# Convolution tails traced in stages, recurrence stages every third step, and the last layer norm's vectors loaded in pieces

## The chip, the cores and the metric

The kernel runs on one core of a Trainium2 chip. The metric is device time in microseconds (us) of the whole program, the median of several runs. TensorE (PE in the profile) multiplies matrices, VectorE (DVE), ScalarE (ACT) and GpSimd (POOL) work elementwise, and the queue of SyncE (SP, SPq where its sequencer issues) issues nearly all DMA loads.

## The reference

One decoder block on 256 tokens of width 2048, in float32:

```python
h = layer_norm(x, emb_ln_g, emb_ln_b)
p = h @ w_in                                   # a, gate, q, f, i, og
u = causal_dwconv(a * sigmoid(gate), conv_w)   # 31 taps, 1024 channels
u = silu(group_layer_norm(u))                  # 8 groups of 128
o = hgrn2_recurrence(silu(q), 1 - fg, i, log(fg))   # 8 heads, fg from f
o = rms_norm(o) * hgrn_norm_g * silu(og)
h = layer_norm(ALPHA * h + concat(u, o) @ w_out, ln1_g, ln1_b)
g, v = split(h @ w_ffn_up)                     # 5632 each
h = layer_norm(ALPHA * h + (silu(causal_dwconv(g)) * v) @ w_ffn_down, ln2_g, ln2_b)
```

## The kernel before

**Weights.** All weights come as 392 blocks of 128 x 1024 floats, 512 KB each, in the order in which they are used. `load_halves` (L97) keeps up to four loads (`raw`, L101) traced ahead on SP's queue. Each block is split into a rounded part `wh` (ScalarE, L124) and a rest `wl` (VectorE, L127), so that products of two rounded halves keep float32's accuracy.

**Products.** `mm_features` (L288) makes 256 features for all tokens from four blocks: `high` (L274) multiplies `wh` with both halves of the input, `low` (L281) `wl` with the high half. `mm_tokens` (L360) makes 512 features with the tokens as the stationary operand, 12 matmuls (L356 to L358) a step of two blocks of the inner dimension.

**Order.** The kernel is written for a scheduler that lays out each engine's instructions ahead of time: the earlier an instruction is traced, the earlier it stands, as far as its inputs are ready by the scheduler's own plan. `high_priority(offset=AHEAD)` moves the weight loads and splits forward in this order.

**The mixer** goes through UNITS, twelve groups of input columns: `ag` (convolution's input and gate), `fq` (forget gate and query of two heads), `v` and `og`. Beside the products runs other work, written as generators that are advanced a stage at a time:

- `conv(p, ups)` (L453): 30 steps of two taps each on VectorE (L462), each yielding a cost of 0.8. Four of them stand in the list `bulk`. When the taps are done, the convolution's tail is put into `later` with a count of LAG = 6.
- `conv_tail(p, y)` (L474): first transposes of the sum (`tp`, TensorE L469 and L472); then statistics (VectorE L484, L486), their root (GpSimd L487, L488) and the normalised tile `tmp` (ScalarE L492); then transposes back, SiLU and the split into `mixhi` and `mixlo`.
- `recurrence(p, ...)` (L529): two heads each; three stages of score products (L469, L472), masks (L573) and decays (L546 to L582), which yield 4.0, then the last scores, the products with `v`, a root-mean-square norm (L626 to L632) and transposes. Four of them stand in the list `chains`.

`pump()` (L159) decides how much of it is traced, and is called four times in `mm_features` and once a step in `mm_tokens`. A credit `turn[1]` grows by RATE = 1.35 a call, at most to 2.7, and falls by the costs that the stages yield. A tail whose count has run out is traced whole. The first recurrence is advanced at every second call, or at every call where `bulk` is empty; what credit is left goes to convolutions, then to a second recurrence. `finish` (L175) drives a generator to its end where its result or its buffers are needed: a convolution before its input tile is written anew, a recurrence before the second next `fq` unit writes its tiles.

The output projection goes over the mixer's channels in three passes (PASSES): the first reads the convolutions' 1024 channels, the second and third the recurrences'. Ahead of the first, `finish` and `run_later` trace what is left of convolutions and tails.

**The feed-forward** makes 44 units (`ffn_up`, L713) of 256 features in two halves of 24 and 20, each followed by four blocks of the down projection. Its tiles take the memory of the mixer's. The last layer norm's vectors are loaded to all partitions, 1 MB each, into `g2` and `b2` (named `g` and `b` in the trace), L733 and L734, ahead of the first unit; they are first read at the very end (`apply`, L736).

Of the kernel before, what the change touches and what calls it, by code (L numbers as in the profile page):

```python
# [18 lines left out]
P = 128  # L19
# [11 lines left out]
RMS_EPS = 1e-6  # L31
AHEAD = 100
LAG = 6
RATE = 1.35
PAD = 368
WARM = 28
# [26 lines left out]
def hybrid_block(ctx, tc, x, wts, par, masks, ident_in, emb_g, emb_b, ln1_g, ln1_b, ln2_g, ln2_b, out):  # L63
    nc = tc.nc
    V, S, G, PE, DMA = nc.vector, nc.scalar, nc.gpsimd, nc.tensor, nc.sync
# [42 lines left out]
    def pc(name, i, n=1):  # L108
        at = PAR[name][0] + i
        return ps_par[:, at:at + n]  # L110
# [34 lines left out]
    chains, bulk, later = [], [], []  # L145
    turn = [0, 0.0]

    def advance(queue, n):

        cost = next(queue[n], None)  # L150
        if cost is None:
            queue.pop(n)
        return cost or 0.0

    def run_later(item):
        later.remove(item)
        turn[1] -= sum(item[1])

    def pump():  # L159


        turn[0] += 1
        turn[1] = min(turn[1] + RATE, 2 * RATE)
        for item in list(later):
            item[0] -= 1
            if item[0] <= 0:
                run_later(item)
        if chains and (turn[0] % 2 == 0 or not bulk):
            turn[1] -= advance(chains, 0)
        while bulk and turn[1] > 0:  # L170
            turn[1] -= advance(bulk, 0)
        if len(chains) > 1 and turn[1] > 0:
            turn[1] -= advance(chains, 1)
# [83 lines left out]
    def residual(gsrc, bsrc, nb, after):  # L257

        cs = slice(nb * 512, (nb + 1) * 512)
        gb = bc.tile([P, 512], F32, name="gb")  # L260
        bb = bc.tile([P, 512], F32, name="bb")
        DMA.dma_start(out=gb, in_=gsrc[cs].partition_broadcast(P))
        DMA.dma_start(out=bb, in_=bsrc[cs].partition_broadcast(P))
        with tc.issue_after(after.ins):
            for t in range(2):
                zz = z[:, t, cs]
                V.scalar_tensor_tensor(zz, zz, ALPHA, gb, ALU.mult, ALU.mult)
                V.scalar_tensor_tensor(zz, bb, ALPHA, zz, ALU.mult, ALU.add)
# [19 lines left out]
    def mm_features():  # L288


        acc, lows = new_acc(), []
        for n, (wh, wl) in enumerate(stream(2)):
            high(acc, wh, n)
            lows.append(wl)
            if n in (1, 2):
                pump()
        for n, wl in enumerate(lows):
            low(acc, wl, n)
            if n in (0, 3):
                pump()  # L300
        return acc
# [26 lines left out]
    def mm_features_by_tile():  # L328


        acc, parts = new_acc(), list(stream(2))

        def tile_of(a, t):
            return a.rearrange("q (h t c) -> q h t c", h=2, t=2)[:, :, t, :]

        for t in range(2):
            for n, (wh, wl) in enumerate(parts):
                for kk in range(4):
                    for j in range(2):
                        PE.matmul(tile_of(acc[j], t), lhsT=wh[:, kk * 256 + j * P:kk * 256 + (j + 1) * P],  # L340
                                  rhs=tile_of(xT[:, 4 * n + kk, :], t), start=t + n + kk == 0, stop=False,
                                  skip_group_check=True)
                if t == 1:
                    low(acc, wl, n)
        return acc

    def add_halves(dst, acc):
        tb = small.tile([P, T], F32, name="tb", bufs=3)
        S.activation(tb, acc[:, T:], AF.Copy)  # L349
        V.tensor_tensor(dst, acc[:, 0:T], tb, ALU.add)  # L350
# [102 lines left out]
    def conv(p, ups):  # L453
# [5 lines left out]
        for k in range(1, TAPS):  # L459
# [4 lines left out]
            yield 0.8  # L464
        later.append([LAG, conv_tail(p, y)])

# [7 lines left out]
    def conv_tail(p, y):  # L474
        tp = ps_tile(4, P)
        together([partial(PE.transpose, tp[:, 2 * i + t], y[i][:, t * P:(t + 1) * P], ident)
                  for i in (1, 0) for t in range(2)])
        yield 0.0
        st = work.tile([P, 4, 6], F32, name="cst", bufs=2)
        mv = work.tile([P, 4, 2], F32, name="cmv", bufs=2)  # L480
        rs = work.tile([P, 4], F32, name="crs", bufs=2)
        zc = work.tile([P, 4, P], F32, name="tmp", bufs=5)
        for j in range(4):
            V.bn_stats(st[:, j], tp[:, j])  # L484
        for j in range(4):
            V.bn_aggr(mv[:, j], st[:, j])  # L486
        G.tensor_scalar(rs, mv[:, :, 1], LN_EPS, None, ALU.add)  # L487
        G.tensor_tensor(rs, rs, mhalf[:, 0:4], ALU.pow)  # L488
        nm = work.tile([P, 4], F32, name="cnm", bufs=2)
        V.scalar_tensor_tensor(nm, mv[:, :, 0], -1.0, rs, ALU.mult, ALU.mult)  # L490
        for j in range(4):
            S.activation(zc[:, j], tp[:, j], AF.Identity, scale=rs[:, j:j + 1], bias=nm[:, j:j + 1])  # L492
        yield 1.2
        tq = ps_tile(4, P)
        together([partial(PE.transpose, tq[:, j], zc[:, j], ident) for j in (3, 0, 1, 2)])
        for i in range(2):
            c = 2 * p + i
            src = tq[:, 2 * i:2 * i + 2].rearrange("q t c -> q (t c)")
            yl = work.tile([P, T], F32, name="cyl", bufs=2)
            S.activation(yl, src, AF.Silu, scale=pc("cn_g", c), bias=pc("cn_b", c))  # L500
            S.activation(mixhi[:, c], yl, AF.Copy)
            mark[0] = V.tensor_tensor(mixlo[:, c], yl, mixhi[:, c].bitcast(F32), ALU.subtract)
# [166 lines left out]
    for k0, k1 in PASSES:  # L669
# [10 lines left out]
        def finish_block(nb, t, acc):  # L680
            zz = z[:, t, nb * 512:(nb + 1) * 512]
            with tc.high_priority():
                V.tensor_tensor(zz, acc, zz, ALU.add)
                if last:
                    V.bn_stats(st1[t][:, nb], zz)
                    if nb == 3:
                        mv, rs = layer_norm_stats(st1[t])
                        normalise(t, mv, rs, minus_mean(mv, rs, V)[0], (V, S, V, S) if t else (S, S, S, S))
                        transpose_split(t, 4 - 2 * t, "ln1_g", "ln1_b")
# [23 lines left out]
    def ffn_up(j, slot):  # L713
        acc = mm_features() if j else mm_features_by_tile()
        g = gpad[j % 3]
        add_halves(g[:, 2:], acc[0])
        vv = fw.tile([P, T], F32, name="vv")
        add_halves(vv, acc[1])
        y = fw.tile([P, T], F32, name="y")
        S.activation(y, g[:, 2:], AF.Identity, scale=pc("fcw", 3 * j + 2), bias=pc("fcb", j))  # L720
        V.scalar_tensor_tensor(y, g[:, 1:1 + T], pc("fcw", 3 * j + 1), y, ALU.mult, ALU.add)  # L721
        V.scalar_tensor_tensor(y, g[:, 0:T], pc("fcw", 3 * j), y, ALU.mult, ALU.add)
        sl = fw.tile([P, T], F32, name="sl")
        S.activation(sl, y, AF.Silu)  # L724
        V.tensor_tensor(vv, sl, vv, ALU.mult)  # L725
        S.activation(acthi[:, slot], vv, AF.Copy)
        mark[0] = V.tensor_tensor(actlo[:, slot], vv, acthi[:, slot].bitcast(F32), ALU.subtract)
# [2 lines left out]
    st2 = [small.tile([P, 4, 6], F32, name="st"), small.tile([P, 8, 6], F32, name="st8")]  # L730
    g2 = ffp.tile([P, D], F32, name="g2")
    b2 = ffp.tile([P, D], F32, name="b2")
    DMA.dma_start(out=g2, in_=ln2_g.partition_broadcast(P))  # L733
    DMA.dma_start(out=b2, in_=ln2_b.partition_broadcast(P))  # L734
    ov = out[0].rearrange("(t p) d -> p t d", p=P)
    def apply(t, mv, rs, blocks):  # L736

# [42 lines left out]
    for half, (j0, j1) in enumerate(HALVES):  # L780
        for j in range(j0, j1):
            ffn_up(j, j - j0)
        for nb in range(4):
            if half == 0:
                residual(ln1_g, ln1_b, nb, mark[0])

            def finish_block(n, t, acc):
                zz = z[:, t, nb * 512:(nb + 1) * 512]
                V.tensor_tensor(zz, acc, zz, ALU.add)
                if half == 1 and t == 0:  # L790
                    V.bn_stats(st2[0][:, nb], zz)
                elif half == 1:
                    for h in range(2):
                        V.bn_stats(st2[1][:, 2 * nb + h], zz[:, h * 256:(h + 1) * 256])

            hi = lambda t, k: acthi[:, k, t * P:(t + 1) * P]
            lo = lambda t, k: actlo[:, k, t * P:(t + 1) * P]
            if (half, nb) == (1, 3):
                mm_tokens_last(hi, lo, j1 - j0)
            else:  # L800
                mm_tokens(hi, lo, j1 - j0, finish_block)
# [79 lines left out]
```

## Time and profile before

| what | value |
|---|---|
| runs | 1169.75, 1171.29, 1172.12 us; median 1171.29 |
| profiled execution | 1171.99 us, its span 1170.2 us |
| TensorE busy | 1141.6 us, 98% of the span |
| VectorE busy | 835.9 us, 71% |
| ScalarE busy | 590.6 us, 50% |
| DMA | 217.75 MB, mean 186 GB/s |

The span is the time from the first to the last instruction in the profile. Busy times of TensorE take modelled ends of matmuls, so neighbouring records overlap; a wait shows as idle time in brackets, with what ended it. The granted clock (PEclk) is a share: 1.00 is 2.4 GHz throughout, 0.50 would be 1.2 GHz.

### The profile page before, as it was taken

How to read it: one execution, taken by the hardware profiler on the slowest of the kernel's cores; microseconds unless marked ns; L12 is line 12 of the kernel's file. 1: busy time of each engine (PE TensorE's matmuls, PEld its weight loads, DVE VectorE, ACT ScalarE, POOL GpSimd, SP SyncE). 2: the span in 40 equal slices, each digit the busy share in tenths (PEclk: the TensorE clock that was granted, in tenths of full speed). 3: DMA queues.
4: the chain of work that ended last, by engine and by line, in shares of the span. 5: the costliest groups of instructions: out<-in, count | busy, mean ns of one | idle time of the engine just before them, and what ended most of it. 6: DMA issues, size and time to landing. Idle time of an engine off the chain costs nothing.

```text
span 1170.2 us, 16117 instructions
## 1 busy us (share of the span) xinstructions
PE 1141.6 (98%) x6066; PEld 984.9 (84%) x6066; DVE 835.9 (71%) x1340; ACT 590.6 (50%) x842; POOL 22.9 (2%) x41
## 2 busy tenths in 40 slices
PE   8999999999999998999999999999999999999996
PEld 7888888888788877888888888888888888888885
DVE  6999999999588686666566578454466666665555
ACT  5755636645544275555555554333445555554330
POOL 1000000000010000000000000000000000000001
PEclk9999999999999999999999999999999999999998
DMA  7665454454547527564564557665554554546651
GB/s 258 219 213 180 150 186 155 159 165 156 184 127 240 173 90 276 176 215 176 184 214 163 200 200 248 199 195 188 175 198 169 208 187 175 215 177 207 194 178 72
DMA packets 61853, 217.75 MB, mean 186 GB/s; under 512 B 6864, under 2 KB 6992, under 8 KB 61520
## 3 DMA queue, kind: packets, MB, share of 16 engines
q1 hardware_dynamic: 61200, 215.69, 55.0%
q8 instruction: 47, 0.77, 0.3%
q10 hardware_dynamic: 576, 1.05, 0.2%
q14 instruction: 30, 0.25, 0.1%
HBM read 214.61 MB, written 2.10 MB: 185 GB/s over the span
## 4 chain that ended last, share of the span: by engine, by line
PE 84%; DVE 10%; DMA 2%; ACT 1%; POOL 1%; issue 1%; SPq 0%; DVEq 0%; ACTq 0%
PE acc L274 33%; PE acc L281 18%; PE acc L357 10%; PE acc L356 10%; PE acc L358 10%; DVE wl L127 3%; DVE y L462 2%; PE ps L472 1%; DMA raw<-in_wts 1%; PE ps L229 1%; DVE A L573 1%; DMA z<-in_x 0%; PE ps L469 0%; DVE z L743 0%; DVE z L740 0%
## 5 line engine op out<-in xcount | busy, mean ns | idle before, releaser
L127 DVE TENSOR_TENSOR wl<-raw,wh 128x1024 fp32r<-128x1024 f32 x392 | 465.4, 1220 | 184.9 <-ACT wh L124 118.5
L124 ACT ACTIVATE wh<-raw 128x1024 fp32r<-128x1024 f32 x392 | 411.9, 1058 | 338.3 <-PE acc L358 175.9
L274 PE MATMUL acc<-xT,wh 128*128 128x512 f32 x1888 | 446.5, 393 | 4.2 <-ACT wh L124 4.2
L274 PEld LDWEIGHTS acc<-xT,wh 128*128 128x128 f32 x1888 | 351.5, 189 | 75.4 <-ACT wh L124 5.1
L281 PEld LDWEIGHTS acc<-xT,wl 128*128 128x128 f32 x1920 | 239.9, 192 | 5.4
L281 PE MATMUL acc<-xT,wl 128*128 128x256 f32 x1920 | 241.5, 283 | 0.0
L356 PE MATMUL acc<-wh,acthi 128*128 128x512 f32 x350 | 136.2, 389 | 0.0
L357 PE MATMUL acc<-wl,acthi 128*128 128x512 f32 x350 | 136.2, 389 | 0.0
L358 PE MATMUL acc<-wh,actlo 128*128 128x512 f32 x350 | 136.2, 389 | 0.0
L349 ACT ACTIVATE tb<-acc 128x256 f32<-128x256 f32 x120 | 39.7, 381 | 129.8 <-PE acc L281 129.7
L462 DVE SCALAR_TENSOR_TENSOR y<-upad,ps_par,y 128x256 f32<-128x256 f32 x240 | 100.8, 477 | 0.1
L358 PEld LDWEIGHTS acc<-wh,actlo 128*128 128x128 f32 x350 | 65.7, 188 | 13.7
L356 PEld LDWEIGHTS acc<-wh,acthi 128*128 128x128 f32 x350 | 65.7, 188 | 13.7
L357 PEld LDWEIGHTS acc<-wl,acthi 128*128 128x128 f32 x350 | 65.7, 188 | 13.3
L721 DVE SCALAR_TENSOR_TENSOR y<-gpad,ps_par,y 128x256 f32<-128x256 f32 x44 | 21.3, 484 | 48.8 <-ACT y L720 48.8
L356 PE MATMUL acc<-wh,xT 128*128 128x512 f32 x128 | 50.8, 397 | 0.0
L356 PE MATMUL acc<-wh,mixhi 128*128 128x512 f32 x128 | 50.5, 395 | 0.0
L357 PE MATMUL acc<-wl,mixhi 128*128 128x512 f32 x128 | 50.5, 394 | 0.0
L358 PE MATMUL acc<-wh,mixlo 128*128 128x512 f32 x128 | 50.2, 392 | 0.0
L358 PE MATMUL acc<-wh,xT 128*128 128x512 f32 x128 | 49.9, 390 | 0.0
L357 PE MATMUL acc<-wl,xT 128*128 128x512 f32 x128 | 49.9, 390 | 0.0
L725 DVE TENSOR_TENSOR vv<-sl,vv 128x256 f32<-128x256 f32 x44 | 18.7, 425 | 33.5 <-ACT sl L724 33.5
(151 smaller groups left out, 748.1 us busy)
## 6 DMA issues: line engine op xcount, KB each, us to landing
raw<-in_wts SPq DMA_DIRECT2D x392, 512.0 KB, 4.2
z<-in_x SPq DMA_DIRECT2D x8, 256.0 KB, 5.0
gb<-in_emb_g SPq DMA_DIRECT2D x4, 256.0 KB, 3.7
bb<-in_emb_b SPq DMA_DIRECT2D x4, 256.0 KB, 4.3
gb<-in_ln_g SPq DMA_DIRECT2D x4, 256.0 KB, 4.0
bb<-in_ln_b SPq DMA_DIRECT2D x4, 256.0 KB, 4.2
g<-in_ln_g SPq DMA_DIRECT2D x1, 1024.0 KB, 7.1
b<-in_ln_b SPq DMA_DIRECT2D x1, 1024.0 KB, 9.2
```

What stands on the lines that cost most here:

```text
L124: return raw, wh, wl, S.activation(wh, raw, AF.Copy)
L127: parts[:] = made, V.tensor_tensor(wl, raw, wh.bitcast(F32), ALU.subtract)
L229: PE.transpose(tp[:, i, n * P:(n + 1) * P], z[:, t, (k0 + i) * P:(k0 + i + 1) * P], ident)
L274: PE.matmul(acc[j], lhsT=wh[:, kk * 256 + j * P:kk * 256 + (j + 1) * P], rhs=xT[:, 4 * n + kk, :], start=n + kk == 0, stop=False, skip_gro ...
L281: PE.matmul(acc[j][:, T:], lhsT=wl[:, kk * 256 + j * P:kk * 256 + (j + 1) * P], rhs=xT[:, 4 * n + kk, 0:T], start=False, stop=4 * n + kk = ...
L349: S.activation(tb, acc[:, T:], AF.Copy)
L356: PE.matmul(acc, lhsT=hi(k + i), rhs=wh[:, cs], start=k + i == 0, stop=False)
L357: PE.matmul(acc, lhsT=hi(k + i), rhs=wl[:, cs], start=False, stop=False)
L358: PE.matmul(acc, lhsT=lo(k + i), rhs=wh[:, cs], start=False, stop=k + i == nk - 1)
L462: V.scalar_tensor_tensor(y[i], ups[i][:, k:k + T], pc("conv_w", c * TAPS + k), y[i], ALU.mult, ALU.add)
L721: V.scalar_tensor_tensor(y, g[:, 1:1 + T], pc("fcw", 3 * j + 1), y, ALU.mult, ALU.add)
L725: V.tensor_tensor(vv, sl, vv, ALU.mult)
```

## The change

Three things change.

A tail in `later` is no longer traced whole when its count has run out: each call at which the count is zero or less traces one stage and sets the count to STEP = 3, until the generator ends. Where `run_later` still traces what is left (ahead of the first output pass), it does so in one go.

The first recurrence in `chains` is advanced only where the credit is above -1.0, and at every third call instead of every second (still at every call where `bulk` is empty, if the credit allows).

The two loads of 1 MB become eight of 256 KB, 512 columns each, kept in a list and traced one behind each of the feed-forward's units 4 to 11, the last columns first. The tiles `g2` and `b2` are still made where they were.

```diff
 LAG = 6
+STEP = 3
 RATE = 1.35
...
         for item in list(later):
             item[0] -= 1
             if item[0] <= 0:
-                run_later(item)
-        if chains and (turn[0] % 2 == 0 or not bulk):
+                item[0] = STEP
+                cost = next(item[1], None)
+                turn[1] -= cost or 0.0
+                if cost is None:
+                    later.remove(item)
+        if chains and turn[1] > -1.0 and (turn[0] % 3 == 0 or not bulk):
             turn[1] -= advance(chains, 0)
...
     g2 = ffp.tile([P, D], F32, name="g2")
     b2 = ffp.tile([P, D], F32, name="b2")
-    DMA.dma_start(out=g2, in_=ln2_g.partition_broadcast(P))
-    DMA.dma_start(out=b2, in_=ln2_b.partition_broadcast(P))
+    last_affine = [(dst, src, slice(n * 512, (n + 1) * 512)) for n in range(4) for dst, src in ((g2, ln2_g), (b2, ln2_b))]
...
         for j in range(j0, j1):
             ffn_up(j, j - j0)
+            if j > 3 and last_affine:
+                dst, src, cs = last_affine.pop()
+                DMA.dma_start(out=dst[:, cs], in_=src[cs].partition_broadcast(P))
```

## Rows read from the trace of the kernel before

**Rows 1.** The page: busy us (share of the span) xinstructions.

```profile
PE 1141.6 (98%) x6066; PEld 984.9 (84%) x6066; DVE 835.9 (71%) x1340; ACT 590.6 (50%) x842; POOL 22.9 (2%) x41
```

**Rows 2.** Chain of waits in order of time: start us, us, what.

```profile
147.19 5.48 PE acc L274 x24
...
453.28 7.28 PE acc L274 x32
...
1046.76 3.83 PE acc L281 x32
```

**Rows 3.** Timeline of TensorE around its waits: start us, us, instruction, idle before.

```profile
114.19 0.33 PE L469 MATMUL ps<-ident,tmp 128*128 128x128 f32 x1 [1.97 <-ACT tmp L492]
...
185.31 0.33 PE L469 MATMUL ps<-ident,tmp 128*128 128x128 f32 x1 [0.78 <-ACT tmp L492]
...
229.79 0.56 PE L469 MATMUL ps<-Q,K 128*128 128x192 f32 x2 [0.98 <-DVE T L549]
...
282.74 0.56 PE L469 MATMUL ps<-Q,K 128*128 128x192 f32 x2 [0.70 <-DVE T L549]
...
320.19 0.33 PE L469 MATMUL ps<-ident,tmp 128*128 128x128 f32 x1 [1.05 <-ACT tmp L492]
...
337.39 0.30 PE L469 MATMUL ps<-ident,tmp 128*128 128x128 f32 x1 [0.40 <-DVE tmp L632]
...
344.81 0.56 PE L469 MATMUL ps<-Q,K 128*128 128x192 f32 x2 [0.20 <-DVE T L549]
...
366.35 0.30 PE L469 MATMUL ps<-ident,tmp 128*128 128x128 f32 x1 [0.31 <-DVE tmp L632]
```

**Rows 4.** Windows: stretch, length, busy us (count) by engine, PEclk, DMA share, GB/s.

```profile
115.00:119.00 4.00, 4.00 (x13) 3.12 (x12) 3.56 (x10) 3.96 (x8) 0.00 (x0) 0.57 0.00 0
...
446.00:450.00 4.00, 4.00 (x14) 3.32 (x14) 3.43 (x3) 3.06 (x3) 0.00 (x0) 0.57 0.55 176
```

**Rows 5.** Chain of waits, 105 to 120 us.

```profile
108.99 0.80 DVE cst L484 x4
...
112.99 1.16 ACT tmp L492 x3
...
114.84 4.11 PE acc L274 x11
```

**Rows 6.** Timeline of SP's queue, 405 to 520 us.

```profile
433.84 0.38 SPq L733 DMA_DIRECT2D g<-in_ln_g  x1
434.27 0.42 SPq L734 DMA_DIRECT2D b<-in_ln_b  x1
```

**Rows 7.** Feed-forward's second unit: TensorE's timeline, then the chain of waits.

```profile
445.78 1.59 PE L274 MATMUL acc<-xT,wh 128*128 128x512 f32 x4 [4.08 <-ACT wh L124]
...
434.84 9.80 DMA raw<-in_wts
...
445.78 3.30 PE acc L274 x8
449.08 4.20 PE acc L281 x32
```

**Rows 8.** DMA issues: KB each, median us from issue to landing.

```profile
raw<-in_wts SPq DMA_DIRECT2D x392, 512.0 KB, 4.2
...
g<-in_ln_g SPq DMA_DIRECT2D x1, 1024.0 KB, 7.1
b<-in_ln_b SPq DMA_DIRECT2D x1, 1024.0 KB, 9.2
```

**Rows 9.** Timeline of SP's queue, 4 to 20 and 366 to 376 us.

```profile
10.12 0.33 SPq L262 DMA_DIRECT2D gb<-in_emb_g  x1
...
371.23 0.33 SPq L262 DMA_DIRECT2D gb<-in_ln_g  x1
```

**Rows 10.** Windows in the mixer, columns as in rows 4.

```profile
230.00:290.00 60.00, 59.30 (x334) 51.95 (x334) 58.96 (x130) 28.38 (x45) 1.17 (x1) 1.00 0.43 142
290.00:345.00 55.00, 53.25 (x262) 43.65 (x261) 38.89 (x82) 28.73 (x52) 5.50 (x5) 1.00 0.54 172
```

## The prediction

> **What bounds the kernel now.** Read the page's first part first. TensorE is busy for 98% of the span, VectorE for 71% [rows 1], so what counts is the time in which TensorE stands still or runs slowly. Next the chain of waits: one product of input features is 32 matmuls in 7.28 us and 32 in 3.83 us, 11.11 us in all, 0.2275 us a wide matmul [rows 2]. The feed-forward's feature products run at that pace from 453.28 us to the last one's end at 1050.59 [rows 2], so there is nothing to win there beyond the first units. What is left stands in the timeline of TensorE, as idle time in brackets with its releaser.
>
> In the mixer there are eight such waits [rows 3], all at L469, the first matmul of a traced group: transposes of a convolution's tail (`tmp` from ACT L492, at 114.19, 185.31 and 320.19), score products of a recurrence stage (`T` from DVE L549, at 229.79, 282.74, 344.81), last transposes of a recurrence (`tmp` from DVE L632, at 337.39, 366.35). The idle times add up to 6.39 us. A matmul's record is 0.39 us long where the next starts after 0.23 us, so each wait costs 0.16 us more than its bracket: 6.39 + 8 x 0.16 = 7.7 us. After the longest, the windows view grants 0.57 in 115:119 [rows 4], part of that stretch at the lower of the two levels (1.2 instead of 2.4 GHz): 11 matmuls took 4.11 us [rows 5] instead of 2.50, another 1.6. The stretches that hold the waits of 0.70 us and 1.05 us were granted 1.00 [rows 10]. **Mixer: 9.3 us to be had.**
>
> In the feed-forward's second unit TensorE stood 4.08 us (4.24 with the overlap) until 445.78 [rows 7]. The chain names the weight load issued at 434.84, which took 9.80 us to land, behind the two vector loads of 1 MB issued at 433.84 and 434.27 [rows 6, 7, 8]. Then the clock fell again, 0.57 in 446:450 [rows 4]: 8 matmuls took 3.30 us instead of 1.82 and the next 32 took 4.20 instead of 3.83 [rows 2, 7], 1.85 us. **Here: 6.1 us.**
>
> **The change part by part.** *Tails and recurrences.* `pump` is called four times in a feature product and once in every 2.73 us (12 matmuls) of a token product. Stepping its arithmetic (RATE, the yielded costs) through UNITS gives the call at which each stage is traced. TensorE keeps to the traced place: the second score group of the first recurrence follows 24 of 32 matmuls [rows 2], the place of the second call of that unit. Tails: before, call 24, 46 and 88 twice, three stages in one go; after, calls 24/27/30, 46/49/52, 80/83/86 and only the last in one go at 88. From the statistics' first instruction at 108.99 to the transposes at 114.19 it took 5.2 us [rows 3, 5]. Three calls are 8.2 us or more, so the waits at 114.19, 185.31 and 320.19 should find their data there; the slack is 3 us. But the last tail is then alone at the head of the first output pass and takes over the wait of 320.19; I keep 1.2 us for it.
>
> Recurrences: before, score groups came every second call (5.5 us of TensorE), after, every third (8.2 us or more) up to the end of the input units; the waits at 229.79 and 282.74 go (1.14 + 0.86). The third recurrence's last stages stand at 92, 95 and 96, so 337.39 goes (0.56). The fourth's stand at 92, 97, 98, 101 to 104, still one call apart in the output pass, where no convolution is left: 344.81 and 366.35 stay (0.36 + 0.47). The second one gets a new wait: at call 76 `finish` for the fourth forget unit finds two of its stages undone and traces them in one go, so that its transposes follow its products by no call at all; by the like waits at 337.39 and 366.35 I take 0.5 us, with 0 and the whole 5.2 us chain as bounds. For waits of other stages that I can't see I allow 0.4 us, bounds 0 and 2. Left over: 1.2 + 0.36 + 0.47 + 0.5 + 0.4 = 2.9. **Mixer: 9.3 - 2.9 = 6.4 us gained**, between 2 and 8.5.
>
> What hides the moved work: VectorE runs 58.96 of 60 us in 230:290, but 38.89 of 55 in 290:345 [rows 10]. Work put off by three calls lands in the second stretch. The fourth recurrence ends at call 104 instead of 99; the output pass that reads it begins at call 112, 21.8 us of matmuls later. No wait is added behind which VectorE's queue stands: the wait for POOL inside a tail is there in both.
>
> *The vectors.* The eight 256 KB loads are traced behind units 4 to 11. Their traced place isn't where they will be issued. The queue of SP is laid out ahead, and a load that waits for nothing is put into the first gap: `gb<-in_emb_g`, traced in the first output pass, was issued at 10.12 us, and the first `gb<-in_ln_g`, traced behind the 24th unit, at 371.23 [rows 9]. The pieces wait for the same memory as `g` and `b` did, free at 433.84. So I expect them from there on, behind weight loads that can be issued, ahead of those that can't. What they get out of it is order: issues stand 0.43 us apart (433.84, 434.27 [rows 6]) and the next weight load was ready at 434.84 [rows 7], so some three pieces go ahead of it and five later, between the next weight loads. Landings of `g` and `b` (433.84 + 7.1 and 434.27 + 9.2 [rows 6, 8]) are 2.5 us apart for 1 MB, 0.62 us for a piece. Five pieces fewer bring that load 3.1 us earlier, and the 4.24 us become 1.1, of a size after which rows 10 show no fall of the clock: **3.1 + 1.85 = 4.9 us gained**. With two ahead it is 5.6, with five 2.4 or so, with all eight 0; at their traced places 6.1, since a unit of 11.11 us has room: its four weight loads, 2 MB, take 5 us at the rate of `g` and `b`, and a piece 0.62.
>
> A rule of the Trainium skill speaks against the pieces. Row first: the two 1 MB loads landed 2.5 us apart [rows 6, 8], though each took over 7 us from issue to landing. The Trainium skill, "DMA: Bandwidth & Descriptors", section "Anatomy of one DMA", gives a transfer (one issued from GpSimd there, from SP here) about 2.0 us of its own beside its bytes, and the section on bandwidth asks for 1 MiB or more. An estimate from that page, were the 2.0 us paid one after the other: 8 x 2.6 us for the pieces instead of 2 x 4.4 us, 12 us more in front of the weights. The rows bear out that such parts overlap, so this keeps a chance of 1 in 100 (below).
>
> **Sum:** 6.4 + 4.9 = 11.3 us. The profiled run took 1171.99 us, 1.8 more than its span; it becomes 1160.7. The median of the runs is 0.7 lower: 1171.3 - 11.3 = **1160.0 us**.
>
> **The rivals.** *All pieces together* (chance 0.30): the eight are laid out in one row before the next weight load. The bytes in front of it are then the same 2 MB, it lands at 444.65 as before or half a us later, wait and slow clock stay. Only the mixer gains: 1171.3 - 6.4 = 1164.9, 1162.5 to 1169. For it: nothing in rows 9 shows how close the plan packs ready loads. Against: the weight load came only 1.0 us after the first vector load.
>
> *At their places* (0.12): something keeps the pieces to units 4 to 11; 1171.3 - 6.4 - 6.1 = 1158.8, down to 1156.5. Against it: rows 9.
>
> *The mixer's waits move instead of going* (0.10): VectorE, full in 230:290 [rows 10], becomes what TensorE waits for; the mixer gains 1 to 3 us, with the pieces' 0 to 4.9: 1164 to 1170.
>
> *Stages in one go leave TensorE empty* (0.04, slower): where two or three stages are traced without a call between, at 76 and at 88, the transposes may be laid directly behind their producers. Then TensorE idles through the chain of 5.2 us and the clock falls for 1.6 more, 6.8 us, twice: 13.6. The other waits are still gone (9.3 - 0.8 that stay = 8.5), so the mixer loses 5.1; with the pieces in one row the time is 1171.3 + 5.1 = 1176.4. It decides from both places being so laid and the pieces bunched; with one of them it comes out near no change. Against it: at call 88 before, two whole tails were traced in one go, and the longest wait there is the 1.2 us of 320.19 [rows 3].
>
> *A piece pays for itself* (0.01, slower): each load's time beyond its bytes, 4.2 us for 512 KB [rows 8] less 1.24 us at the rate of `g` and `b`, about 3 us, in a row: six loads more, 18 us: 1171.3 - 6.4 + 18 = 1183.
>
> **How the numbers follow.** Forecast 0.43 (1157.5 to 1162.5), bunched 0.30, at their places 0.12, waits moved 0.10, slower ones 0.05. The range runs from 1156.5, below the third case, to 1167.5, which leaves out the slower cases, the upper end of the moved waits and a little of the bunched one. A measurement of this kernel can tell about 0.2%, 2.3 us, from no change: faster is below 1169.0. All of the first three cases lie there but for some hundredths, of the fourth most: 0.88; within 0.2%: 0.07; slower: 0.05.
>
> **What would show it.** Right: no idle at L469 from ACT L492 before the output pass; a granted clock of 1.00 around 115; score groups without a wait for `T` up to call 88; one wait of about a us at the head of the output pass; the pieces on SP's queue from about 423 to 440 us, mixed with weight loads; a wait of 1 to 2 us in the second feed-forward unit. Wrong: pieces issued one a unit from 490 us on; all eight in a row with the 4 us wait still there; a wait of more than 2 us behind the products of the second recurrence; TensorE waiting for `wl` in the mixer.

## The result, and the profile after

| | before | after |
|---|---|---|
| median of four runs each | 1170.90 us | 1163.26 us |
| lowest to highest | 1169.75 to 1172.12 | 1162.45 to 1164.34 |
| profiled run / its span | 1171.99 / 1170.2 | 1164.34 / 1162.5 |

The ratio of after to before is 0.9935, with a 95% interval of 0.9918 to 0.9952: 7.6 us faster, where 11.3 us were forecast. The page shows TensorE 2.3 us less busy than in [rows 1]:

```profile
PE 1139.3 (98%) x6066; PEld 985.0 (85%) x6066; DVE 835.0 (72%) x1340; ACT 586.3 (50%) x840; POOL 21.2 (2%) x41
```

Where the gain was made shows in the chain of waits (each piece of work followed back to what released it), at places that both kernels have. (Line numbers of after are 5 higher in the mixer: L469 is L474, L549 is L554, L632 is L637, L274 is L279.) The first fence is the chain of before at the mixer's end, the first statistics of a row block of the last token product; the second is the chain of after, at that place, at the head of the feed-forward's third product (453.28 us in [rows 2]) and at its end (1046.76 us there). Columns are start us, us, what.

```profile
408.32 0.70 DVE z L683
```

```profile
406.92 0.70 DVE z L688
...
445.50 7.28 PE acc L279 x32
...
1038.99 3.83 PE acc L286 x32
```

At the mixer's end after is 1.40 us ahead (408.32 - 406.92). At the third product it is 7.78 us ahead (453.28 - 445.50), and at the last one still 7.77 (1046.76 - 1038.99). So the mixer gave 1.4 us where 6.4 were forecast, and the first two units of the feed-forward gave 6.4 where 4.9 were forecast. Everything behind them is unchanged.

The two executions already differ ahead of the first tail, in code that the change doesn't touch. TensorE's timelines have the first token product here, before and then after:

```profile
62.81 0.40 PE L356 MATMUL acc<-wh,xT 128*128 128x512 f32 x1
```

```profile
63.26 0.40 PE L361 MATMUL acc<-wh,xT 128*128 128x512 f32 x1
```

From there to the mixer's end it took 345.51 us and 343.66, so the mixer's gain between these two profiles is 1.4 us by the end and 1.85 by the length.

The waits of TensorE in the mixer of after, from its timeline (idle time before the instruction in brackets, with its releaser), answer to [rows 3]:

```profile
237.34 0.56 PE L474 MATMUL ps<-Q,K 128*128 128x192 f32 x2 [1.79 <-DVE T L554]
...
247.26 0.56 PE L474 MATMUL ps<-Q,K 128*128 128x192 f32 x2 [0.19 <-DVE T L554]
...
275.67 0.30 PE L474 MATMUL ps<-ident,tmp 128*128 128x128 f32 x1 [2.91 <-DVE tmp L637]
...
320.18 0.39 PE L363 MATMUL acc<-wh,mixlo 128*128 128x512 f32 x1
320.66 0.33 PE L474 MATMUL ps<-ident,tmp 128*128 128x128 f32 x1
...
352.29 0.56 PE L474 MATMUL ps<-Q,K 128*128 128x192 f32 x2 [0.71 <-DVE T L554]
```

None of the three long waits for a tail's `tmp` is left. The last tail, alone at the head of the output pass, starts 0.48 us behind the matmul before it, 0.25 more than the usual step. In their place stand two long waits inside the input units that were not there: 1.79 us for `T`, and 2.91 us behind the second recurrence's products. The windows view (stretch, length, busy us and count of PE, PEld, DVE, ACT, POOL, then PEclk, DMA share, GB/s) answers to [rows 4, 10]:

```profile
115.00:119.00 4.00, 4.00 (x34) 3.99 (x33) 2.75 (x11) 3.43 (x7) 1.42 (x2) 1.00 0.26 100
230.00:290.00 60.00, 55.11 (x285) 46.62 (x284) 53.17 (x111) 29.73 (x47) 1.91 (x1) 0.97 0.49 159
277.00:281.00 4.00, 4.00 (x12) 3.11 (x12) 1.20 (x3) 3.99 (x7) 0.00 (x0) 0.57 0.51 159
437.00:460.00 23.00, 23.00 (x133) 20.29 (x132) 17.22 (x22) 14.69 (x21) 0.00 (x0) 1.00 0.93 283
```

The slow clock at 115 is gone, but it stands behind the 2.91 us wait now (0.57 in 277:281). In the feed-forward TensorE is busy for all of 437:460 at 1.00. VectorE's idle time in 230:290 lies behind 262: in 230:262, around the wait for `T`, it is busy for all 32.00 us. The chain of after around the 2.91 us wait:

```profile
268.83 1.14 DVE wl L128
...
270.67 0.49 DVE y L467
271.16 1.13 DVE wl L128
272.29 0.09 DVE oss L631
...
272.45 1.92 POOL oss L632
...
274.67 0.87 DVE tmp L637 x3
...
275.67 0.30 PE ps L474
...
276.30 6.84 PE acc L279 x23
```

The norm at L631 is the next step of the recurrence. Ahead of it VectorE took convolution taps (`y`) and weight splits (`wl`). Then TensorE's 23 matmuls took 6.84 us instead of 23 x 0.2275 = 5.23: the slow clock cost 1.6 us more.

The feed-forward's gain of 6.38 us adds up from three things that before has in the second unit: the wait of 4.08 us [rows 7] with its 0.16 of overlap, the slow clock behind it, 1.85, and a shorter wait just ahead of it, 0.17 with 0.16 of overlap, 6.4 together. The row of the shorter one, from TensorE's timeline of before:

```profile
439.59 2.11 PE L274 MATMUL acc<-xT,wh 128*128 128x512 f32 x8 [0.17 <-ACT wh L124]
```

Last, SP's queue, which answers to [rows 6]:

```profile
432.00 20.03 SPq L102 DMA_DIRECT2D raw<-in_wts  x12
452.12 0.38 SPq L789 DMA_DIRECT2D b<-in_ln_b  x1
...
453.97 1.20 SPq L789 DMA_DIRECT2D b<-in_ln_b  x1
...
461.03 0.44 SPq L789 DMA_DIRECT2D g<-in_ln_g  x1
```

The pieces (L789) were issued five in a row from 452.12 and three from 461.03, ahead of their traced places, but behind the weight loads on which the second unit had waited.

### The profile page after: what moved, and what is told of

Its sections match the earlier page's. It is cut to its first block, busy times and chain, and to the rows that moved or that the text cites. A ratio compares the mean times of both kernels' runs of the same rounds, so it can differ in the third digit from the quotient of the medians.

```text
span 1162.5 us, 16118 instructions
## 1 busy us (share of the span) xinstructions
PE 1139.3 (98%) x6066; PEld 985.0 (85%) x6066; DVE 835.0 (72%) x1340; ACT 586.3 (50%) x840; POOL 21.2 (2%) x41
## 4 chain that ended last, share of the span: by engine, by line
PE 81%; DVE 15%; issue 1%; POOL 1%; ACT 1%; DMA 1%; SPq 0%; DVEq 0%; POOLq 0%
PE acc L279 33%; PE acc L286 18%; PE acc L363 10%; PE acc L361 9%; PE acc L362 9%; DVE wl L128 4%; DVE y L467 4%; DVE A L578 1%; PE ps L477 1%; PE ps L234 1%; DMA z<-in_x 1%; DVE z L747 0%; DVE z L744 0%; PE acc L345 0%; POOL oss L632 0%
## 5 line engine op out<-in xcount | busy, mean ns | idle before, releaser
L279 PE MATMUL acc<-xT,wh 128*128 128x512 f32 x1888 | 443.5, 391 | 0.0
L279 PEld LDWEIGHTS acc<-xT,wh 128*128 128x128 f32 x1888 | 351.2, 189 | 70.6
```

Source lines behind the costliest of these rows:

```text
L279: PE.matmul(acc[j], lhsT=wh[:, kk * 256 + j * P:kk * 256 + (j + 1) * P], rhs=xT[:, 4 * n + kk, :], start=n + kk == 0, stop=False, skip_gro ...
```

## The experiments

Two questions were put. Which half of the change made the gain, and by what: the place of the vectors' loads or their size? And what do the two new waits in the mixer come from? All kernels compute the whole reference. Where two kernels were run in separate series, their ratios to before are compared. A kernel's mixer is timed in its profile from the first token product to the mixer's end, and the rest from there to the end of the span.

**One half each.** First before with only the loads changed:

```diff
-    DMA.dma_start(out=g2, in_=ln2_g.partition_broadcast(P))
-    DMA.dma_start(out=b2, in_=ln2_b.partition_broadcast(P))
+    last_affine = [...]          # as in after
...
+            if j > 3 and last_affine:
+                dst, src, cs = last_affine.pop()
+                DMA.dma_start(out=dst[:, cs], in_=src[cs].partition_broadcast(P))
```

> The kernel before with only the eight pieces behind units 4 to 11; tails and recurrences as before. Theory (the two parts don't touch each other): the 4.1 us wait in the second feed-forward unit and the slow clock behind it go, 6.3 us; the mixer's eight waits stay. 1170.9 - 6.3 = 1164.6 us. Rival (the pieces' part needs the mixer's new order, which brings the last passes to that place at another moment): a wait of 1 to 4 us stays in the second unit, 1166 to 1171.

Measured: 1164.35 us, ratio 0.9943 (0.9930 to 0.9955). No wait is left in the second feed-forward unit. 6.8 us, nearly the whole gain of the change, come from the loads alone, close to the 6.3 expected.

Then after with the two loads of 1 MB put back where they were:

```diff
-    last_affine = [...]
+    DMA.dma_start(out=g2, in_=ln2_g.partition_broadcast(P))
+    DMA.dma_start(out=b2, in_=ln2_b.partition_broadcast(P))
...
-            if j > 3 and last_affine:
-                ...
```

> The changed kernel with the two 1 MB loads where the kernel before has them; only tails and recurrences are changed. Theory: the mixer as a whole gave 1.5 to 2 us, since 4.7 us came back behind the second recurrence's products and 2 us at its second score group; 1169.0 us, with the 4 us wait in the second feed-forward unit as before. Rival (the mixer's part is worth what was forecast and the rest was lost in the feed-forward): 1164.5.

Measured: 1170.74 us, ratio 0.9993 (0.9984 to 1.0002), no change that can be measured. The mixer's half by itself is worth 0.4 us by the medians, with an interval of -0.2 to 1.9; 1169.0 us had been expected. Part of the mixer's gain is lost again in the feed-forward: its wait is back and longer than the 4.08 of before, and the rest of the program takes 762.5 us instead of 761.9. TensorE's timeline:

```profile
443.36 2.07 PE L279 MATMUL acc<-xT,wh 128*128 128x512 f32 x4 [4.46 <-ACT wh L125]
```

**The loads: place or size.** Two kernels tell it apart, each the opposite of the other: eight small loads at the old place, and two whole loads at a late one.

```diff
+    while last_affine:           # at the old place, ahead of the feed-forward
+        dst, src, cs = last_affine.pop()
+        DMA.dma_start(out=dst[:, cs], in_=src[cs].partition_broadcast(P))
...
-            if j > 3 and last_affine:
-                ...
```

> The changed kernel with the same eight 256 KB loads, but all traced where the kernel before traced its two 1 MB loads, ahead of the first feed-forward unit. Theory (the traced place decides: it puts the loads behind the weight loads that are traced before them, and the size of a load is of no account): they go out in one row at about 433 us, the wait of 4 to 5 us in the second unit and the slow clock behind it are back, 1163.3 + 6.3 = 1169.6 us. Rival (small loads let weight loads pass between them): a wait of 1 to 2 us, 1164 to 1166.

Measured: 1173.95 us, ratio 1.0019 (1.0008 to 1.0030), a little slower than before, where 1169.6 were expected. The profiled execution is the fastest of ten, 1170.44 us, so the rows show the mechanism and not the whole loss. Rows of SP's queue, of the chain of waits, and of TensorE's timeline, one fence each:

```profile
429.74 0.37 SPq L741 DMA_DIRECT2D b<-in_ln_b  x1
...
432.53 1.18 SPq L741 DMA_DIRECT2D b<-in_ln_b  x1
433.75 1.63 SPq L741 DMA_DIRECT2D g<-in_ln_g  x1
```

```profile
435.48 7.52 DMA raw<-in_wts
```

```profile
444.13 3.62 PE L279 MATMUL acc<-xT,wh 128*128 128x512 f32 x8 [7.00 <-ACT wh L125]
```

Traced early, the pieces stand in one row, and TensorE waits 7.00 us instead of the 4.46 of the whole loads. The weight load that TensorE waits for was issued at 435.48, 5.74 us behind the first piece. With whole loads (the one-half kernel above) it went out 1.00 us behind the first of them, by SP's queue and the chain of waits:

```profile
431.50 0.37 SPq L738 DMA_DIRECT2D g<-in_ln_g  x1
431.92 0.42 SPq L739 DMA_DIRECT2D b<-in_ln_b  x1
```

```profile
432.50 9.72 DMA raw<-in_wts
```

So the load was late because the issues ahead of it took long: six of 0.37 to 0.43 us, then 1.18 and 1.63. It landed faster (7.52 us instead of 9.72), which gave back 2.2 of the 4.74 us. Why the seventh and eighth issue took so long the trace doesn't tell.

```diff
+            if j == 4:
+                DMA.dma_start(out=g2, in_=ln2_g.partition_broadcast(P))
+                DMA.dma_start(out=b2, in_=ln2_b.partition_broadcast(P))
...
-            if j > 3 and last_affine:
-                ...
```

> The changed kernel with the two whole 1 MB loads traced behind the feed-forward's fifth unit instead of eight pieces behind units 4 to 11. Theory (place, not size): they are issued at about 452 us in the gap in which the pieces went, the weight loads behind them find their buffers late anyway, no wait of TensorE: 1163.3 us, the same as the changed kernel. Rival (pieces are what spares the weight loads): 2 MB in one row delay the weight loads behind them by 2 us more than five pieces did, a wait of 1 us or more in the third or fourth unit: 1164.5 to 1169.

Measured: 1161.99 us, ratio 0.9919 (0.9903 to 0.9936), no wait in the feed-forward. The interval overlaps that of after (0.9918 to 0.9952). SP's queue:

```profile
449.80 0.38 SPq L787 DMA_DIRECT2D g<-in_ln_g  x1
450.23 0.42 SPq L788 DMA_DIRECT2D b<-in_ln_b  x1
```

The profiles settle what the intervals leave open. Behind the mixer's end the eight kernels with late loads, whole or in pieces, take 755.4 to 755.7 us; with two whole loads at the old place it is 761.9 (before) and 762.5, with eight pieces there 764.4. The place decides, and the cutting into pieces does nothing for the gain.

**The mixer: the wait behind the second recurrence's products.** The forget unit that drives an older recurrence to its end now stops once that recurrence has read its tiles, which is all that the unit's new tiles need:

```diff
-        if p >= 2:
-            finish(chains, recs[p - 2])
+        while p >= 2 and recs[p - 2] in chains and p - 2 not in past:
+            advance(chains, 0)
...
         S.activation(a01, sp[:, T:].rearrange("q (a t) -> q a t", a=2), AF.Copy)
+        past.add(p)
```

> The changed kernel, but ahead of the fourth forget unit the second recurrence is driven only until it has read its tiles (its last score products), not to its end: its norm and transposes are then traced at the next third calls, no longer in one go. Theory (tracing two stages in one go costs the idle time of 2.9 us at 275.67 and the slow clock behind it): 4.7 us gone, 1158.5 us, and the granted clock 1.00 at 277. Rival (VectorE is the bound there, the wait moves to the next group of score products or to the head of the output pass): 1161 to 1164.

Measured: 1159.82 us, ratio 0.9902 (0.9887 to 0.9917), below the interval of after. The wait and its slow clock are gone, by the window where they stood:

```profile
274.00:278.00 4.00, 4.00 (x19) 3.34 (x18) 2.81 (x7) 2.69 (x5) 1.01 (x1) 1.00 0.84 263
```

That is 3.4 us by the medians, 3.9 by the ratios and 4.0 by the mixer's length (343.66 and 339.61 us), where the profile of after made it 4.7. The rest is a tail's wait that came back, 0.87 us at 315.23; the medians may differ further because the slow clock isn't there in every execution (last section). The wait for `T` stays (1.84 us at 238.48).

**The wait for `T`.** VectorE's timeline of after, with the score products behind which it starts ending on TensorE at 227.21:

```profile
225.82 3.65 DVE L467 SCALAR_TENSOR_TENSOR y<-upad,ps_par,y 128x256 f32<-128x256 f32 x9
229.38 1.22 DVE L128 TENSOR_TENSOR wl<-raw,wh 128x1024 fp32r<-128x1024 f32 x1
...
231.55 0.72 DVE L571 COPY_PREDICATED A<-mk,ps 128x512 f32<-128x512 uint32 x1
...
232.63 1.22 DVE L128 TENSOR_TENSOR wl<-raw,wh 128x1024 fp32r<-128x1024 f32 x1
...
235.20 1.25 DVE L128 TENSOR_TENSOR wl<-raw,wh 128x1024 fp32r<-128x1024 f32 x1
...
237.12 0.20 DVE L554 TENSOR_TENSOR T<-T 128x32 f32<-128x32 f32 x1
```

The stage's first instruction (L571) came 4.3 us after its products. Taps and a split went first, and two more splits stood between its own instructions. If that order is the cause, putting the stage's instructions further ahead must take the wait away, with nothing else changed against the last kernel:

```diff
+            with tc.high_priority(offset=40):
                 if n == 0:
                     V.copy_predicated(a, ...)
                 ...                       # the whole VectorE part of a stage
```

> The kernel in which the second recurrence is only driven until it has read its tiles, and in addition VectorE's part of a recurrence stage (masks and decays) stands 40 instructions further ahead in the tracing order, so that two weight splits of 1.2 us no longer stand between a stage's score products and its decays. Theory (the 2.0 us wait at 236 us comes from VectorE's order, the splits ahead of the decays): that wait goes, nothing else comes: 1157.9 us. Rival (VectorE is full there, 59 of 60 us, and what it puts off is missed elsewhere): 1159.5 to 1161, with a new wait for wl or at another score group.

Measured: 1157.56 us, ratio 0.9885 (0.9870 to 0.9900), the fastest of all versions, 5.7 us below after. VectorE now finishes `T` ahead of the two splits that stood between the stage's instructions, and TensorE's wait there is gone:

```profile
230.78 0.72 DVE L572 COPY_PREDICATED A<-mk,ps 128x512 f32<-128x512 uint32 x1
...
233.88 0.45 DVE L554 TENSOR_TENSOR T<-T 128x32 f32<-128x32 f32 x1
234.03 1.35 DVE L128 TENSOR_TENSOR wl<-raw,wh 128x1024 fp32r<-128x1024 f32 x1
```

The stage's first instruction (230.78) still comes 4.2 us behind its products, which end at 226.61, so the taps and the split ahead of it stayed: what took the wait away is the two splits of 1.2 us each. What is left in the input units is one wait of 0.50 us for `Q`; the output pass has two, 0.87 us for a tail's `tmp` and 0.43 for `T`. Against the last kernel the time is 2.3 us less by the medians, but the two intervals overlap (0.9887 to 0.9917, 0.9870 to 0.9900); by the mixer's length it is 1.8 us (339.61 and 337.79). VectorE is as full there as before, 4.00 of 4.00 us in 235:239: it has no more time, but spends it first on what TensorE waits for, and no wait for `wl` appears in exchange.

**Tails against recurrences.** After with the recurrences at every second step and no bound on the credit, the tails staged:

```diff
-        if chains and turn[1] > -1.0 and (turn[0] % 3 == 0 or not bulk):
+        if chains and (turn[0] % 2 == 0 or not bulk):
```

> The changed kernel with recurrences advanced as in the kernel before, at every second call and without the credit's bound; tails in stages and pieces as changed. Theory (the tails' stages are what gains in the mixer, the recurrences' third step costs): waits at 114 and 185 us and the slow clock behind the first go, 4.7 us; the recurrences' waits of 0.9 and 1.1 us stay, nothing is traced in one go at the fourth forget unit: 1170.9 - 6.3 - 4.7 = 1160 us. Rival (the third step is what takes the waits away): 1163 or more.

Measured: 1164.43 us, ratio 0.9942 (0.9929 to 0.9954), the same as with only the loads changed. The tails' waits at 114 and 185 us are gone (one of 1.04 us stays at the head of the output pass, 318.26), yet others stand in the timeline of TensorE, at 150.30 (1.16 us) and here:

```profile
227.87 0.56 PE L474 MATMUL ps<-Q,K 128*128 128x192 f32 x2 [2.22 <-DVE T L554]
```

I had expected 1160. The time is that of the rival, 1163 or more, though not for its reason: the tails' waits went without the third step, and came up again as waits for `T`. The kernel without the lump, with tails traced whole, is the last corner of the square:

```diff
-                item[0] = STEP
-                cost = next(item[1], None)
-                ...
+                run_later(item)
```

> The kernel in which the second recurrence is only driven until it has read its tiles, recurrences at every third call and pieces as changed, but tails traced whole as in the kernel before. With the run that has staged tails and recurrences at every second call this completes the square of the two halves of the mixer's change. Theory (the halves help only together, since each alone leaves VectorE's bursts in the way of the other's groups): waits of 1.7 and 1 us at 112 and 183 us are back, perhaps with the slow clock: 1162.5 to 1164.5 us. Rival (the third step alone is the gain, the tails' stages are worth nothing): 1160.

Measured: 1162.07 us, ratio 0.9921 (0.9906 to 0.9937). The tails' waits are back:

```profile
114.64 0.33 PE L470 MATMUL ps<-ident,tmp 128*128 128x128 f32 x1 [1.46 <-ACT tmp L493]
```

Three more stand at 184.29, 288.60 and 316.25 (0.86, 1.09 and 0.92 us). But no score group in the input units waits for `T` here, where the kernel with staged tails waits 1.84 us at 238.48. VectorE's timeline has that `T` here with whole tails, and then with staged ones:

```profile
237.72 0.20 DVE L550 TENSOR_TENSOR T<-T 128x32 f32<-128x32 f32 x1
```

```profile
238.26 0.19 DVE L554 TENSOR_TENSOR T<-T 128x32 f32<-128x32 f32 x1
```

Counted from the first token product (63.77 and 64.32) it ends at 174.15 and 174.13 us, the same moment. With the recurrences at every second step it is the same again, 164.96 us with whole tails (loads changed alone) and 164.74 with staged ones, and TensorE's wait for it grows from 0.99 to 2.22 us. So up to there VectorE sets the pace: the time that TensorE no longer loses at the tails it loses at the next `T`.

The square, all with the late loads: neither half 0.9943, tails alone 0.9942, recurrences alone (without the lump) 0.9921, both (without the lump) 0.9902. By themselves the staged tails gain nothing, for the reason just read. Beside the recurrences' third step they seem to (0.9921 to 0.9902), but these two intervals overlap, so that gain isn't settled (by the mixer's length 341.16 and 339.61 us, one profile each). Whole tails with the stage put first were not run.

**A distance of two.** The kernel without the lump with `STEP = 2`:

> The kernel in which the second recurrence is only driven until it has read its tiles, with the stages of a convolution's tail two calls apart instead of three (STEP = 2). Theory (a tail's statistics and norm take 5.2 us and more where VectorE is full, two calls are 5.5 us): the waits behind the first two or three tails come back in part, 0.5 to 2 us each, perhaps with the slow clock: 1161 to 1164. Rival (any distance will do): 1159.8 as with three.

Measured: 1161.48 us, ratio 0.9913 (0.9898 to 0.9928); the interval overlaps that of three steps (0.9887 to 0.9917). No tail's wait came back in its profile that three steps don't have too (0.86 us at 315.36, 0.87 there), against my expectation, so two calls are enough there. Its profile has a slow clock behind a wait for `T` (0.60 in 238:242) that the other lacks; whether the distance itself costs anything stays open.

## Why the prediction was right or wrong

The time, 1163.26 us, lies in the range and on the forecast side, 3.3 us above the point. Two errors stand against each other: the mixer gave 5 us less than forecast, the feed-forward 1.5 more. That the time came so near is luck in that part. Of the signs of being right two came, no wait for a tail ahead of the output pass and a clock of 1.00 around 115; the others didn't, and one sign of being wrong did: more than 2 us behind the second recurrence's products.

**Tails: right on the spot, wrong on what it is worth.** The waits at 114.19, 185.31 and 320.19 are gone, and the slow clock at 115 with them. The 1.2 us kept for the last tail is 0.25 in after; in four later kernels with staged tails it is 0.86 to 1.04 and 0.16 of overlap. But I booked the waits at 114.19 and 185.31 as gain, and the square shows that most of it is waited for again at the next `T`.

**Recurrences: the step that failed.** "The waits at 229.79 and 282.74 go" and "I take 0.5 us" for the stages traced in one go. What was left over:

| left over in the mixer | forecast us | after us (bracket + 0.16 each) |
|---|---|---|
| last tail, 320.66 | 1.2 | 0.25 |
| input units' score groups, 237.34 and 247.26 | 0.4 (allowance) | 2.3 |
| second recurrence in one go, 275.67 | 0.5 | 3.1, and 1.6 of slow clock |
| fourth recurrence, 352.29 (366.35 is gone) | 0.83 | 0.87 |
| sum | 2.9 | 8.1 |

9.3 - 8.1 = 1.2 us, against 1.4 to 1.85 read from the profiles. Two terms failed, the 0.4 us for "waits of other stages" and the 0.5.

For the first I counted how much TensorE work lies between two stages and took VectorE's 5.2 us chain as given; "No wait is added behind which VectorE's queue stands" is the sentence that failed. The third step by itself did what I had forecast: with whole tails no score group of the input units waits. With staged tails TensorE gets there earlier and VectorE doesn't. [Rows 10] showed VectorE full there, and I gave the rival that rests on it, the waits that move, 0.10. In its mixer term (1 to 3 us) that rival was right. The order of VectorE's queue decides what a full VectorE delays: the kernel with the stage put first took the wait away by two splits. For the second term I took the middle of the like waits at 337.39 and 366.35, which lie in the output pass, where there are no taps. No row of before shows a stage in one go inside the input units; the bounds 0 and 5.2 held. The rival "stages in one go leave TensorE empty" came true at one of its two places, at 4.7 us instead of 6.8, and not at call 88. The profile of after is one draw. The mixers of four kernels that share its mixer code ended, by the first statistics as above, at 406.92 (after), 405.98 (early whole loads), 404.23 (early pieces) and 404.79 (late whole loads), those of the old mixer at 408.32 (before) and 406.89 (loads changed alone). By the means of these, 405.5 and 407.6, the mixer's gain is 2.1 us; by the means of the mixer's length, 343.2 and 344.7, it is 1.4.

**Feed-forward: right on what stood in the way, wrong on where the pieces go, its size short by 1.5 us.** I expected the pieces "from there on", from 433.84, with some three ahead of the second unit's weight load. They were issued behind it, from 452.12, so the whole 4.24 us of the wait and the 1.85 of slow clock went: 6.1 by my own price for that case, 6.4 measured; the last 0.3 is the wait at 439.59, which I had left out. The right step was that the issue place isn't the traced one. Its error was to take the first gap after the memory comes free for the place. Whole loads behind unit 4 came to 449.80, so a load traced later is also issued later, if not as late as it is traced.

Bunching was the rival to which I gave 0.30, with the wait as before or half a us more. At the old place it happened, and cost 2.5 us of wait beyond the whole loads (7.00 against 4.46 in one profile each), 3.2 by the medians. On the rule of the Trainium skill, "DMA: Bandwidth & Descriptors", section "Bandwidth", to batch to 1 MiB: in front of the weights the whole loads were the better by those 2.5 to 3.2 us, not by the 12 us of the estimate in which the 2.0 us of its section "Anatomy of one DMA" are paid one after the other; behind them size made no difference that shows.

## What to carry to other kernels

A wait on TensorE that ends with another engine's chain isn't cured by putting more TensorE work ahead of it while other work stands inside that chain: look at the order of that engine's queue between the producer's end and the releaser, and move the chain ahead there. Taking away one wait of TensorE while the other engine sets the pace only moves it to the next thing that engine makes. Code that drives older work to its end before new tiles are taken should stop at the last read of those tiles; here that was worth 3.4 us. The order of the queue gave some 2 more (1159.82 to 1157.56, with intervals that overlap, and 1.8 by the mixer's length). Loads that nobody needs soon belong behind those that are waited for, and their size then matters little.

## What the runs showed of the hardware that was not expected

A wait of TensorE is followed by the lower clock in one execution and not in the next. The wait of 2.91 us at 275.67 in after was followed by 0.57. The same wait in the kernel with whole late loads was longer, and the clock stayed, by TensorE's timeline and the windows behind it:

```profile
275.05 0.30 PE L474 MATMUL ps<-ident,tmp 128*128 128x128 f32 x1 [2.94 <-DVE tmp L637]
```

```profile
275.00:279.00 4.00, 3.95 (x20) 3.34 (x21) 2.56 (x5) 3.25 (x6) 0.00 (x0) 1.00 0.61 187
279.00:283.00 4.00, 4.00 (x28) 3.69 (x27) 1.08 (x2) 3.85 (x5) 0.00 (x0) 1.00 0.17 65
```

The tail's wait of 1.97 us at 114.19 in before [rows 3] was followed by 0.57 [rows 4], that of 1.54 at 114.01 with only the loads changed by 1.00 in 113:117. After's four runs fall into two pairs, 1162.45 and 1162.48 us (granted clock 0.996 over the span in both), and 1164.03 and 1164.34 (0.993 and 0.994). The distance of about 1.7 us is that of one such stretch (1.6 us), but the start alone varies as much: over the eleven profiles the first token product begins between 61.28 and 64.32 us, with 1.00 granted in 14:18 in the earliest and 0.50 in the latest. Which of the two parts the pairs is open. A forecast by one profile should count a slow clock that follows a wait as a chance, not as a fixed price.

The second is how long an issue can take: of eight loads of 256 KB in a row the first six took 0.37 to 0.43 us each on SP's queue, the seventh 1.18 and the eighth 1.63, so the next load went out 5.74 us behind the first of them, and 1.00 us behind the first of two loads of 1 MB. In after the fifth of five pieces in a row, at 453.97, took 1.20.
